# Another order of the side work in an attention unit, and the softmax shift on VectorE

## The chip, the cores and the metric

The kernel runs on one core of one Trainium2 chip. The time is the device time of one execution in microseconds; the figure that counts is the median of several runs. A core has five engines with a queue each: TensorE (PE in the profile; its weight loads are PEld), VectorE (DVE), ScalarE (ACT), GpSimd (POOL) and SyncE (SP), which here only issues DMAs. Each engine works off its own queue in order, and waits at the head of the queue until what the next instruction needs is there.

## The reference

One transformer-like block on x of 256 tokens by 2048 features, in float32:

```python
h = _rmsnorm(x, norm1_g)
proj = h @ w_in                        # q (12 heads), k and v (4 heads), u (512)
a = _rmsnorm(_window_attention(q, k, v, sink), attn_out_g)
f = _rmsnorm(_fourier_mix(u, w_fourier), fourier_out_g)
x = x + jnp.concatenate([a, f], axis=-1) @ w_out
x = x + _conv_ffn(_rmsnorm(x, norm2_g), w_up, dw_w, dw_b, w_down)
return _rmsnorm(x, normf_g)
```

Three query heads share one key head. The softmax of a head has one further logit, the head's `sink`, that takes part in the maximum and in the sum but weighs no value:

```python
scores = jnp.where(valid, q @ k.T * HEAD_DIM ** -0.5 - slope * abs(rel), NEG_INF)
m = jnp.maximum(jnp.max(scores, axis=-1, keepdims=True), sink_b)
p = jnp.exp(scores - m)
p = p / (jnp.sum(p, axis=-1, keepdims=True) + jnp.exp(sink_b - m))
out = p @ v
```

## The kernel before, in words

**Products in two parts.** Every weight block of 1 MB is loaded by SP (`load`, L161), then split (`split`, L174): ScalarE writes the high part `hi` (L181), VectorE the rest `lo` = raw - hi (L182), and TensorE multiplies the parts. Split runs two blocks ahead of TensorE; there are three raw buffers and three of each part, and the load of block i+3 is issued by SP behind the split of block i.

**Units.** One weight block is one *unit* of work. `unit(i)` (L382) writes, in this order: the small products set down in `before[i]` and the unit's 32 or 24 large matmuls on TensorE; the side work `beside[i]` on the other engines; the split of block i+2 (`step`, L362); and the side work `behind[i]`. The tables are filled by `at(...)`, and what is entered first for a unit is written first. The schedule is manual: the order in which the program is written is the order in each engine's queue. Units 0 to 3 are u, 4 to 7 v, 8 to 23 q and k (`QK_ORDER`: k0, q0, q1, q2, k1, q3, ... q11, so units 8, 12, 16 and 20 are keys), 24 to 39 the output projection. Then come the feed-forward units, which the change does not touch.

**One query head's way** (loop at L762; a head's unit is n = 0):

- n = 1, `qk_out` (L629): ScalarE copies the second half of the unit's PSUM bank (`tmp_q`, L631), VectorE adds the halves (`add_q`, L633); a key's sum is also scaled (`add_k`, L635). `qk_parts` (L638): ScalarE writes the high part of `qT` (L269) or `kT` (L643), VectorE the low part (L270, L644).
- n = 2, `scores` (L649): six matmuls `ps_s` on TensorE, ahead of the unit's own. `scores_out` (L662): VectorE adds the distances and takes each row's maximum in one instruction per half (L670); GpSimd makes the exponentials' shift in two (L674, L675). Then, in `behind`, `exps` (L678): ScalarE's two exponentials (L684) and the sink's (L688), and GpSimd's sum (L689).
- n = 3, `weigh` (L692): VectorE's reciprocal (L694) and two scalings (L697). For heads 0 to 9 also `flip_out` (L720): VectorE transposes 32 by 32 blocks (L314), and SP writes them to HBM in four DMAs.
- n = 4, `flip_in` (L726): SP reads them back, turned (`flop`). For heads 10 and 11 instead `turn` (L699) on TensorE and `turn_out` (L710).
- n = 6, `flip_parts` (L731): the probabilities `pt` in two parts, on ScalarE (L739) and VectorE (L740).
- n = 7 (heads 10 and 11: 5), `values` (L743): matmuls `ps_o`, ahead of the unit's own; `values_out` (L757): ScalarE's square (L486) and high part `cat` (L269), VectorE's low part (L270), GpSimd's running sum of squares (L490).

So the side work of one unit serves up to five heads at different stages. Since a key's unit takes the place of a query's once in four, units with i mod 4 = 2 have no scores and no `flip_parts`, and those with i mod 4 = 3 no `weigh` and no `values_out`.

Before the change the side work of a unit stands in this order: `flip_parts`, `weigh` and `flip_out`, `flip_in`, `qk_out`, `values_out`, `turn_out`, `scores_out`, `qk_parts`; then the split, then `exps`.

Of the kernel before, what the change touches and what calls it, by code (L numbers as in the profile page):

```python
# [8 lines left out]
F32 = mybir.dt.float32  # L9
F32R = mybir.dt.float32r  # L10
AF = mybir.ActivationFunctionType
ALU = mybir.AluOpType

P = 128
# [4 lines left out]
NH = 12  # L19
# [19 lines left out]
V_G2, V_GA, V_GF, V_DW, V_DB, V_SINK = 0, 16, 28, 32, 161, 204  # L39
V_N = 216  # L40


def slopes():
    def pow2(n):
        start = 2.0 ** (-8.0 / n)
        return [start ** (i + 1) for i in range(n)]

    return pow2(8) + pow2(16)[0::2][: NH - 8]
# [7 lines left out]
FLIPS = range(NH - 2)  # L56
# [48 lines left out]
def block_kernel(  # L105
# [19 lines left out]
    nc = tc.nc  # L125
    SL = slopes()
# [9 lines left out]
    def bank(pool, name):  # L136
        return pool.tile([P, 512], F32, tag=pool.name, name=name)
# [62 lines left out]
    rel = cat_pool.tile([P, 512], F32, tag="cat", name="rel")  # L200
# [16 lines left out]
    def u_part(k, o, n, m=1):  # L217

        rows = ux[k // 4][:, (k < 4) * U_HEAD :].rearrange("p (k c) -> p k c", k=4)
        return rows[:, k % 4 : k % 4 + m, o : o + n]  # L220
# [39 lines left out]
    ps = bank(dn, "ps_warm")  # L260
# [3 lines left out]
    def vcol(o, n=1):  # L264
        return vec[:, o : o + n]
# [107 lines left out]
    before, beside, behind = {}, {}, {}  # L373

    def at(when, i, f, *a):
        when.setdefault(i, []).append((f, a))
# [17 lines left out]
    for k in range(NK):  # L394
# [3 lines left out]
        n = 1 if c < 2 else 2  # L398
# [3 lines left out]
        if q % n == 0:  # L402
            w, h = u_part(k, 0, FW, n), hi[:, q : q + n, :]
# [20 lines left out]
    ph = pa.enter_context(tc.tile_pool(name="pa", bufs=1))  # L424
# [5 lines left out]
    rq_neg = ph.tile([P, 2], F32, tag="rq_neg", name="rq_neg")  # L430
    rq_pos = ph.tile([P, 2], F32, tag="rq_pos", name="rq_pos")
    rq_inv = ph.tile([P, 2], F32, tag="rq_inv", name="rq_inv")
    sink_neg = ph.tile([P, NH], F32, tag="sink_neg", name="sink_neg")

    def token_sums(c):
        for b in range(2):
# [150 lines left out]
    def distances():  # L587

        for b in range(2):
            s = slice(b * S, (b + 1) * S)  # L590
            nc.vector.tensor_scalar(rel[:, s], rel[:, s], rq_inv[:, b : b + 1], None, ALU.mult)
        nc.vector.tensor_scalar(sink_neg, vcol(V_SINK, NH), -1.0, None, ALU.mult)

    at(beside, 5, fourier_positions)
    at(before, 6, fourier_weights)
# [3 lines left out]
    at(beside, 7, fourier_rows_out)  # L599
    at(beside, 8, lambda: rows_out(v_hi, v_lo, ps_v))  # L600
    at(behind, 8, distances)

    def fourier_channels_steps():
# [22 lines left out]
    qk_sb, st = {}, {}  # L626
    sq_a = ph.tile([P, S], F32, tag="sq", name="sq_a")

    def qk_out(kind, h, ps):  # L629
        tmp = ph.tile([P, S], F32, tag="tmp", name=f"tmp_{kind}{h}", bufs=2)  # L630
        nc.scalar.activation(tmp, ps[:, S : 2 * S], AF.Copy)  # L631
        add = ph.tile([P, S], F32, tag="add", name=f"add_{kind}{h}", bufs=2)
        nc.vector.tensor_tensor(add, ps[:, 0:S], tmp, ALU.add)  # L633
        if kind == "k":
            nc.vector.tensor_tensor(add, add, r1b, ALU.mult)  # L635
        st["add", kind, h] = add
# [25 lines left out]
    def scores_out(h):  # L662

        ps = st.pop(("s", h))
        sc = ph.tile([P, 512], F32, tag="sc", name=f"sc{h}", bufs=4)
        mx = ph.tile([P, 2], F32, tag="mx", name=f"mx{h}", bufs=2)
        neg = ph.tile([P, 2], F32, tag="neg", name=f"neg{h}", bufs=2)
        for b in range(2):
            s = slice(b * S, (b + 1) * S)
            nc.vector.tensor_tensor_reduce(  # L670
                sc[:, s], ps[:, s], rel[:, s], -float(SL[h]), -3e38, ALU.add,
                ALU.max, mx[:, b : b + 1],
            )
        nc.gpsimd.tensor_tensor(neg, mx, rq_neg, ALU.mult)  # L674
        nc.gpsimd.tensor_scalar(neg, neg, sink_neg[:, h : h + 1], None, ALU.min)  # L675
        st["sc", h] = sc, neg

    def exps(h):  # L678
# [83 lines left out]
    for i in range(N_QK, N_OUT + 8):  # L762
        heads = {i - s: h for (kind, h), s in slot_of.items() if kind == "q"}
        new = [kh for kh, s in slot_of.items() if i - s == 1]
        for n, h in sorted(heads.items()):
            if n == 5 + 2 * (h in FLIPS):
                at(before, i, values, h)
        if 4 in heads and heads[4] not in FLIPS:
            at(before, i, turn, heads[4])
        if 2 in heads:  # L770
            at(before, i, scores, heads[2])
        if 6 in heads and heads[6] in FLIPS:
            at(beside, i, flip_parts, heads[6])
        if 3 in heads:
            at(beside, i, weigh, heads[3])
            if heads[3] in FLIPS:
                at(beside, i, flip_out, heads[3])
        if 4 in heads and heads[4] in FLIPS:
            at(beside, i, flip_in, heads[4])
        for kind, h in new:  # L780
            at(beside, i, lambda k=kind, h=h: qk_out(k, h, st.pop(("ps", k, h))))
        for n, h in sorted(heads.items()):
            if n == 5 + 2 * (h in FLIPS):
                at(beside, i, values_out, h)
        if 4 in heads and heads[4] not in FLIPS:
            at(beside, i, turn_out, heads[4])
        if 2 in heads:
            at(beside, i, scores_out, heads[2])
        for kind, h in new:
            at(beside, i, qk_parts, kind, h)  # L790
        if 2 in heads:
            at(behind, i, exps, heads[2])

# [85 lines left out]
    for n, (c, kq) in enumerate(OUT_ORDER):  # L879
        i = N_OUT + n  # L880
# [14 lines left out]
        if kq >= 2:  # L895
            part = "a" if kq == 2 else "f"
            ps = ps_a[c] if kq < 3 else ps_a[c, "f"]
# [315 lines left out]
    for q in range(2):  # L1213
        kind, j = items[q]
        ps = bank(mm, f"ps_{kind}{j}")
# [15 lines left out]
    for n, it in enumerate(items):  # L1231
# [8 lines left out]
        if it[0] in ("gate", "val"):  # L1240
            kind, j = it
            ps = bank(mm, f"ps_{kind}{j}")
# [4 lines left out]
        if it[0] == "product":  # L1247
            kind, g, c, p = it
# [3 lines left out]
            elif end and p in ("P2", "N4"):  # L1252
                ps = joined[c, p] = bank(mm, f"ps_{p}{g}{c}")
                by_parts(ps, parts[p], *halves.pop(it), GROUPS[g][1], True, False)
            else:
                ps = bank(mm, f"ps_{p}{g}{c}")
# [5 lines left out]
        else:  # L1262
            kind, c = it
            hi, lo = halves.pop(up_index[n])
            if c < 2:
                ps = [joined.pop((c, p)) for p in ("P2", "N4")]
            else:
                ps = [bank(mm, f"ps_l{c}{b}") for b in range(2)]
# [10 lines left out]
    i = up_index[n]  # L1279
# [158 lines left out]
```

## Time and profile before

| what | value |
|---|---|
| median of 3 runs | 941.33 us (941.06 to 941.93) |
| profiled execution | 941.03 us, its span 938.9 us |
| mean granted TensorE clock | 0.997 |
| busy share of the span: PE, DVE, ACT, POOL | 99%, 82%, 57%, 8% |
| attention's query and key units (8 to 23) | from 53.6 to 158.5 us of the span |

The span goes from the first to the last instruction of the profiled execution; the device time has about 2 us around it. The profile's views used here: the page with busy times and the chain that ended last; the waits (which engine stood still for whom); the timeline (instructions in order of time, with the idle time before them in brackets and what ended it); groups of instructions by line and shape (busy time, mean ns of one, idle time before); and windows (busy time of each engine in a stretch).

### The profile page before, as it was taken

To read this page: it belongs to the slowest core of one execution; us is meant where nothing else is said; L and a number is where in the kernel's file an instruction comes from. 1 tells how busy PE (TensorE), PEld (TensorE's weight loads), DVE (VectorE), ACT (ScalarE), POOL (GpSimd) and SP (SyncE) were. 2 spreads that over 40 slices of the span, in tenths; PEclk is the share of its full clock that TensorE was granted. 3 is DMA by queue.
4 is the path that set the end of the run, shared out by engine and by line. 5 is a ranking of instruction groups with operands and counts; after the bars stand their busy time and mean duration, and the time that the engine had idled before them with its cause. 6 is when DMAs were issued, how large, how long until landed. Compare 5 with 4: busy or idle time off the path is not lost.

```text
span 938.9 us, 12849 instructions
## 1 busy us (share of the span) xinstructions
PE 928.0 (99%) x5005; PEld 803.5 (86%) x5005; DVE 765.5 (82%) x945; ACT 539.6 (57%) x672; POOL 72.9 (8%) x104
## 2 busy tenths in 40 slices
PE   9999999999999999999999999999999999999996
PEld 7888888888888888888888888888888888888885
DVE  7657888778677777798888997878979789989986
ACT  7755666645554555566555665556655556655553
POOL 0102222300000000000000000000000000000002
PEclk9999999999999999999999999999999999999998
DMA  9965767557757668887797778777787978779652
GB/s 367 309 224 169 231 196 236 193 174 281 243 221 232 177 227 238 278 269 239 220 296 252 246 216 286 237 262 232 260 248 240 309 224 269 241 233 273 194 179 90
DMA packets 55148, 223.25 MB, mean 238 GB/s; under 512 B 21136, under 2 KB 25744, under 8 KB 31536
## 3 DMA queue, kind: packets, MB, share of 16 engines
q1 hardware_dynamic: 50544, 192.94, 56.8%
q0 software_dynamic: 4544, 29.49, 16.9%
q8 instruction: 39, 0.64, 0.3%
q14 instruction: 21, 0.17, 0.1%
HBM read 216.13 MB, written 6.29 MB: 237 GB/s over the span
## 4 chain that ended last, share of the span: by engine, by line
PE 95%; DVE 2%; ACT 1%; issue 1%; DMA 0%; POOL 0%; DVEq 0%; POOLq 0%; ACTq 0%
PE ps_val L350 25%; PE ps_gate L350 25%; PE ps_q L350 5%; PE ps_P L1148 3%; PE ps_P L1149 3%; PE ps_P L1147 3%; PE ps_N L1148 3%; PE ps_N L1149 3%; PE ps_N L1147 3%; PE ps_k L350 2%; PE ps_a L333 2%; PE ps_a L335 2%; PE ps_a L334 2%; PE ps_s L654 1%; PE ps_ff L333 1%; PE ps_ff L335 1%
## 5 line engine op out<-in xcount | busy, mean ns | idle before, releaser
L182 DVE TENSOR_TENSOR lo<-raw,hi 128x2048 fp32r<-128x2048 f32 (+1 forms) x129 | 293.5, 2275 | 53.9 <-ACT hi L181 53.6
L181 ACT ACTIVATE hi<-raw 128x2048 fp32r<-128x2048 f32 (+1 forms) x129 | 245.3, 1902 | 36.7 <-PE ps_a L334 14.6
L350 PE MATMUL ps_val<-hU,hi 128*128 128x512 f32 x688 | 236.2, 389 | 0.0
L350 PE MATMUL ps_gate<-hU,hi 128*128 128x512 f32 x688 | 236.2, 389 | 0.0
L350 PE MATMUL ps_val<-hU,lo 128*128 128x256 f32 x688 | 189.9, 276 | 0.0
L350 PE MATMUL ps_gate<-hU,lo 128*128 128x256 f32 x688 | 189.9, 276 | 0.0
L350 PEld LDWEIGHTS ps_gate<-hU,hi 128*128 128x128 f32 x688 | 129.1, 188 | 26.8
L350 PEld LDWEIGHTS ps_val<-hU,hi 128*128 128x128 f32 x688 | 129.1, 188 | 26.8
L350 PEld LDWEIGHTS ps_gate<-hU,lo 128*128 128x128 f32 x688 | 129.1, 188 | 1.3
L350 PEld LDWEIGHTS ps_val<-hU,lo 128*128 128x128 f32 x688 | 129.1, 188 | 1.3
L922 ACT ACTIVATE ft_g<-ps_gate 128x256 f32<-128x256 f32 x43 | 16.5, 384 | 123.0 <-PE ps_gate L350 123.0
L922 ACT ACTIVATE ft_v<-ps_val 128x256 f32<-128x256 f32 x43 | 16.5, 384 | 91.5 <-PE ps_val L350 91.5
L350 PE MATMUL ps_q<-hT,hi 128*128 128x512 f32 x192 | 65.1, 391 | 0.0
L1147 PE MATMUL ps_P<-hi_P,op_P 128*128 128x512 f32 x144 | 56.0, 389 | 0.0
L1148 PE MATMUL ps_P<-hi_P,op_P 128*128 128x512 f32 x144 | 56.0, 389 | 0.0
L1149 PE MATMUL ps_P<-lo_P,op_P 128*128 128x512 f32 x144 | 56.0, 389 | 0.0
L350 PE MATMUL ps_q<-hT,lo 128*128 128x256 f32 x192 | 51.2, 277 | 0.0
L1039 DVE TENSOR_TENSOR lo_N<-sumw,hi_N 128x2048 fp32r<-128x2048 f32 (+1 forms) x20 | 41.5, 2077 | 9.4 <-ACT hi_N L1038 9.2
L1147 PE MATMUL ps_N<-hi_N,op_N 128*128 128x512 f32 x108 | 42.0, 389 | 0.0
L1148 PE MATMUL ps_N<-hi_N,op_N 128*128 128x512 f32 x108 | 42.0, 389 | 0.0
L1149 PE MATMUL ps_N<-lo_N,op_N 128*128 128x512 f32 x108 | 42.0, 389 | 0.0
L350 PEld LDWEIGHTS ps_q<-hT,hi 128*128 128x128 f32 x192 | 35.2, 188 | 6.6
(389 smaller groups left out, 1598.9 us busy)
## 6 DMA issues: line engine op xcount, KB each, us to landing
raw<-in_w_up SPq DMA_DIRECT2D x86, 1024.0 KB, 5.6
raw<-in_w_in SPq DMA_DIRECT2D x20, 1024.0 KB, 5.3
raw<-in_w_out SPq DMA_DIRECT2D x16, 1024.0 KB, 4.9
sumw<-in_w_down POOLq DMA_DIRECT2D x16, 1024.0 KB, 8.7
raw<-in_w_down_late SPq DMA_DIRECT2D x4, 1024.0 KB, 7.0
raw<-in_w_down_last SPq DMA_DIRECT2D x4, 768.0 KB, 4.2
turnp<-flip SPq DMA_DIRECT2D x40, 64.0 KB, 2.9
flop<-turnp SPq DMA_DIRECT2D x10, 256.0 KB, 4.7
```

The source lines that it names most:

```text
L181: nc.scalar.activation(hi[:, 0:n], raw[:, 0:n], AF.Copy)
L182: nc.vector.tensor_tensor(lo[:, 0:n], raw[:, 0:n], f32(hi[:, 0:n]), ALU.subtract)
L333: nc.tensor.matmul(ps, ah, wh, start=first and q == q0, stop=False)
L334: nc.tensor.matmul(ps, al, wh, start=False, stop=False)
L335: nc.tensor.matmul(ps, ah, wl, start=False, stop=last and q == q0 + len(kk) - 1)
L350: nc.tensor.matmul(ps[:, x], (hi, lo)[i][:, k * P : (k + 1) * P], hk(k)[:, x], start=n == 0 and k == 0, stop=n == len(order) - 1 and k == ...
L654: nc.tensor.matmul(ps[:, b * S : (b + 1) * S], qT[:, qo + b * P : qo + (b + 1) * P], kT[:, ko : ko + S], start=n == 0, stop=n == 2,)
L922: nc.scalar.activation(tmp, ps[:, S : 2 * S], AF.Copy)
L1039: nc.vector.tensor_tensor(lo, src, f32(hi), ALU.subtract)
L1147: nc.tensor.matmul(ps, o[:, 0, p, :], hi[:, s], start=first and p == 0, stop=False)
L1148: nc.tensor.matmul(ps, o[:, 1, p, :], hi[:, s], start=False, stop=False)
L1149: nc.tensor.matmul(ps, o[:, 0, p, :], lo[:, s], start=False, stop=last and p == n - 1)
```

## The change

Three things are changed, all in the attention units.

- The order of the side work becomes: `qk_out`, `flip_parts`, `qk_parts`, `values_out`, `weigh` and `flip_out`, `flip_in` or `turn_out`, `scores_out`; then, as before, the split and `exps`.
- The running maximum of the scores begins with the sink's logit, divided by the row's query scale once at the setup (`sink_least`, two products of 12 columns in `distances`, in place of the negated sinks), and no longer with -3e38.
- The shift `neg` is then the maximum times `rq_neg`, one VectorE instruction; GpSimd's product and its minimum with the negated sink are gone.

```diff
-    sink_neg = ph.tile([P, NH], F32, tag="sink_neg", name="sink_neg")
+    sink_least = [ph.tile([P, NH], F32, tag="sink0", name="sink0"), vcol(V_N, NH)]
...
-        nc.vector.tensor_scalar(sink_neg, vcol(V_SINK, NH), -1.0, None, ALU.mult)
+        for b in range(2):
+            nc.vector.tensor_scalar(
+                sink_least[b], vcol(V_SINK, NH), rq_inv[:, b : b + 1], None, ALU.mult
+            )
...
             nc.vector.tensor_tensor_reduce(
-                sc[:, s], ps[:, s], rel[:, s], -float(SL[h]), -3e38, ALU.add,
-                ALU.max, mx[:, b : b + 1],
+                sc[:, s], ps[:, s], rel[:, s], -float(SL[h]), sink_least[b][:, h : h + 1],
+                ALU.add, ALU.max, mx[:, b : b + 1],
             )
-        nc.gpsimd.tensor_tensor(neg, mx, rq_neg, ALU.mult)
-        nc.gpsimd.tensor_scalar(neg, neg, sink_neg[:, h : h + 1], None, ALU.min)
+        nc.vector.tensor_tensor(neg, mx, rq_neg, ALU.mult)
...
+        for kind, h in new:
+            at(beside, i, lambda k=kind, h=h: qk_out(k, h, st.pop(("ps", k, h))))
         if 6 in heads and heads[6] in FLIPS:
             at(beside, i, flip_parts, heads[6])
+        for kind, h in new:
+            at(beside, i, qk_parts, kind, h)
+        for n, h in sorted(heads.items()):
+            if n == 5 + 2 * (h in FLIPS):
+                at(beside, i, values_out, h)
         if 3 in heads:
             at(beside, i, weigh, heads[3])
             if heads[3] in FLIPS:
                 at(beside, i, flip_out, heads[3])
-        if 4 in heads and heads[4] in FLIPS:
-            at(beside, i, flip_in, heads[4])
-        for kind, h in new:
-            at(beside, i, lambda k=kind, h=h: qk_out(k, h, st.pop(("ps", k, h))))
-        for n, h in sorted(heads.items()):
-            if n == 5 + 2 * (h in FLIPS):
-                at(beside, i, values_out, h)
-        if 4 in heads and heads[4] not in FLIPS:
-            at(beside, i, turn_out, heads[4])
+        if 4 in heads:
+            at(beside, i, flip_in if heads[4] in FLIPS else turn_out, heads[4])
         if 2 in heads:
             at(beside, i, scores_out, heads[2])
-        for kind, h in new:
-            at(beside, i, qk_parts, kind, h)
```

## The prediction

> **What bounds the kernel now.** I read the page first (busy times, then the chain that ended last), then the waits of TensorE, then the timeline of the attention stage engine by engine.
>
> ```profile
> span 938.9 us, 12849 instructions
> PE 928.0 (99%) x5005; PEld 803.5 (86%) x5005; DVE 765.5 (82%) x945; ACT 539.6 (57%) x672; POOL 72.9 (8%) x104
> PE 95%; DVE 2%; ACT 1%; issue 1%; DMA 0%; POOL 0%; DVEq 0%; POOLq 0%; ACTq 0%
> PE ps_s L654 <- ACT qT L269: 1.4, 2, 0.9
> ACT qT L269 <- DVE add_q L633: 27.4, 12, 3.0
> ```
>
> The reader is to see that TensorE is busy for 99% of the span and is 95% of the chain: time is saved only where TensorE itself stands still. The fourth line is the one wait for another engine that it has in the middle of the program: twice the scores (ps_s) wait for the high part of qT, 1.4 us. The fifth says why: ScalarE, which writes that part, waits in front of it for VectorE's sum add_q in each of 12 heads. A matmul that waits inside a group is merged into the group's length, so the chain in order of time has to be read too:
>
> ```profile
> 90.26 5.58 PE ps_q L350 x32
> 95.83 1.11 PE ps_s L654 x6
> 96.94 5.48 PE ps_q L350 x32
> 102.42 0.72 PE ps_o L749 x6
> 103.14 0.72 PE ps_s L654 x6
> ...
> 129.60 0.72 PE ps_o L749 x6
> ...
> 157.07 0.72 PE ps_o L749 x6
> ```
>
> The columns are start, length and what ran. Six score matmuls take 0.72 us undisturbed (103.14) and 1.11 at 95.83. In the timeline of TensorE two more groups are long, 1.19 and 1.20 us, with pure idle time in front, in brackets. These three are the scores of heads 3, 6 and 9, the first query head of each later key group, ahead of units 15, 19 and 23. VectorE's and ScalarE's rows in unit 18 then show how it comes about:
>
> ```profile
> 122.94 1.19 PE L654 MATMUL ps_s<-kT,qT 128*128 128x256 f32 x6 [0.54 <-ACT qT L269]
> 150.43 1.20 PE L654 MATMUL ps_s<-kT,qT 128*128 128x256 f32 x6 [0.85 <-ACT qT L269]
> ```
> ```profile
> 117.93 2.29 DVE L182 TENSOR_TENSOR lo<-raw,hi 128x2048 fp32r<-128x2048 f32 x1 [0.87 <-ACT hi L181]
> 120.31 0.17 DVE L694 RECIPROCAL ex<-sm 128x2 f32<-128x2 f32 x1
> 120.51 0.86 DVE L697 TENSOR_SCALAR sc<-sc,ex 128x256 f32<-128x256 f32 x2
> 121.41 0.71 DVE L314 STREAM_TRANSPOSE flip<-sc 128x512 f32<-128x512 f32 x1
> 122.05 0.39 DVE L633 TENSOR_TENSOR add_q<-ps_q,tmp_q 128x256 f32<-128x256 f32 x1
> 122.36 0.47 DVE L270 SCALAR_TENSOR_TENSOR cat<-ps_o,vec,cat 128x256 fp32r<-128x256 f32 x1
> 122.92 0.42 DVE L270 SCALAR_TENSOR_TENSOR qT<-add_q,qT 128x256 fp32r<-128x256 f32 x1
> 124.72 2.29 DVE L182 TENSOR_TENSOR lo<-raw,hi 128x2048 fp32r<-128x2048 f32 x1 [1.38 <-ACT hi L181]
> ```
> ```profile
> 119.16 0.36 ACT L631 ACTIVATE tmp_q<-ps_q 128x256 f32<-128x256 f32 x1
> 122.47 0.42 ACT L269 ACTIVATE qT<-add_q 128x256 fp32r<-128x256 f32 x1 [2.32 <-DVE add_q L633]
> ```
>
> VectorE leaves the previous unit's weight split at 120.22 (117.93 + 2.29). It then does the softmax weighting and the transpose (120.31 to 122.05) ahead of add_q, though ScalarE's copy that add_q needs has been there since 119.52. ScalarE idles 2.32 us, qT's high part starts at 122.47, the low part ends at 123.34, and TensorE, free since 122.40 (122.94 - 0.54), waits for both. Behind it, VectorE waits 1.38 us for ScalarE's `hi`, which could not start before qT.
>
> **The stall's size.** Ahead of unit 19: 0.54 + (1.19 - 0.72) = 1.01 us. Ahead of unit 23: 0.85 + (1.20 - 0.72) = 1.33. Ahead of unit 15: (1.11 - 0.72) + (5.58 - 5.48) = 0.49. Sum 2.83 us. A second way: from 102.42 to 129.60 and on to 157.07 are 27.18 and 27.47 us; four units of 5.47 with three value groups and three score groups of 0.72 need 26.2, so 1.0 and 1.3 are lost. This is all that TensorE loses in attention, 0.3% of the run.
>
> **The change part by part.**
>
> *The sum of q or k and its parts first.* Nothing is added; add_q or add_k moves ahead of weighting and transpose, and the two parts of qT or kT ahead of values_out, weighting and scores. Take unit 18 with VectorE as late as now: add_q starts at 120.22 and ends at 120.61 (0.39), the high part ends at 121.1 (0.42 and some 0.05 to hand over), the low part at 121.5. TensorE asks at 122.40, so 0.9 us are to spare. Unit 22 and unit 14 by the same steps:
>
> ```profile
> 145.41 2.29 DVE L182 TENSOR_TENSOR lo<-raw,hi 128x2048 fp32r<-128x2048 f32 x1 [0.87 <-ACT hi L181]
> 90.97 2.29 DVE L182 TENSOR_TENSOR lo<-raw,hi 128x2048 fp32r<-128x2048 f32 x1 [1.26 <-ACT hi L181]
> ```
>
> Unit 22: free at 147.70, qT whole at 149.0, asked for at 149.58 (150.43 - 0.85): 0.6 to spare. Unit 14: 93.26, 94.6, 95.83: 1.2. So all three stalls go even if nothing else gets better. **Term: -2.83 us.**
>
> What is late next? At the start of unit 19 TensorE needs scores, the values' operand and the split weights. The weights' low part for unit 19 ended at 120.22, for a start at 122.40 with a score group in front. In units 14, 18 and 22 no probabilities have to be unpacked (the head there would be a key's place), so nothing stands between. In other units the unpacking (pt) moves behind add_q, later by 0.4 us, and gates the next unit's value matmuls. In unit 19:
>
> ```profile
> 126.93 0.75 DVE L740 TENSOR_TENSOR pt<-flop,pt 128x256 fp32r<-128x256 f32 x2
> ```
>
> It ended at 127.68 and was wanted at 129.60: 1.9 to spare, 1.5 after the move.
>
> *The backlog itself.* ScalarE's `hi` now follows qT, the square and `cat`, all early, while VectorE still has weighting, transpose and scores to do. The 0.87 to 1.38 us that VectorE waits for `hi` in each unit should mostly go, so it runs less late, and the margins above grow. I take no time for this, as TensorE does not see it.
>
> *Scores' maximum last, the shift on VectorE.* Per head two GpSimd instructions go and one small VectorE product comes:
>
> ```profile
> L670 DVE CUSTOM_DVE_ANT_0 sc<-ps_s,rel 128x256 f32<-128x256 f32 x24 | 9.1, 417 | 0.0
> L674 POOL TENSOR_TENSOR neg<-mx,rq_neg 128x2 f32<-128x2 f32 x12 | 5.6, 467 | 49.0 <-DVE mx L670 49.0
> L675 POOL TENSOR_SCALAR neg<-neg,sink_neg 128x2 f32<-128x2 f32 x12 | 4.0, 332 | 1.2
> L592 DVE TENSOR_SCALAR sink_neg<-vec 128x12 f32<-128x12 f32 x1 | 0.2, 165 | 0.0
> L1183 DVE CUSTOM_DVE_ANT_0 z_P<-xs,ssq 128x256 f32<-128x256 f32 x1 | 0.5, 485 | 0.5 <-POOL ssq L1324 0.5
> 96.90:158.50 61.60, 60.20 (x374) 53.78 (x373) 50.06 (x102) 39.92 (x87) 14.37 (x26) 1.00 0.71 217
> ```
>
> The product has the shape of the reciprocal at 120.31 (two columns): 0.17 us, with the step to the next instruction 0.2. A maximum that begins with a value per row instead of a constant is not in the trace at this place; its nearest row is L1183, the same instruction begun from a column, 485 against 417 ns: 0 to 0.07 us each, two per head, and I take 0 since L1183 also reads both operands from SBUF. So VectorE gains 0.2 to 0.34 us per head, at most 12 x 0.34 = 4.1 us. The cover is in the last row (columns: span, then busy time of PE, PEld, DVE, ACT, POOL): from 96.90 to 158.50 VectorE is busy 50.06 of 61.60, so 11.5 us are free, and nine heads take 3.1 at most. **Term: 0.** If the cover were gone, the heads' 2 to 4 us would stand on the end.
>
> Behind the maximum nothing waits but ScalarE's exponentials, which come after `hi` anyway, and VectorE's split, which it reaches 0.2 us later. On GpSimd the shift needs 0.7 us and once much more:
>
> ```profile
> 170.50 2.18 POOL L674 TENSOR_TENSOR neg<-mx,rq_neg 128x2 f32<-128x2 f32 x1 [2.17 <-DVE mx L670]
> 173.10 0.60 ACT L684 ACTIVATE sc<-sc,neg,rq_pos 128x256 f32<-128x256 f32 x1 [3.61 <-POOL neg L675]
> ```
>
> There VectorE's 2.29 us split ran at the same time, and ScalarE lost 3.61 us; TensorE went on, so its removal is worth nothing by itself. The Trainium skill says why, in "SBUF — State Buffer", section "Who interferes with whom": a VectorE instruction with two SBUF inputs and a GpSimd instruction that reads SBUF exclude each other, and whichever came first holds the port to its end. This trace agrees, 2.18 us against the usual 0.31.
>
> *Weighting and transpose later in the unit.* What they feed: the transpose's four DMAs on SP, the read-back a unit later, its unpacking two units after that. SP's order within a unit stays (write, read back, then the weights' load). In unit 18 the transpose ended at 122.12; with add_q, qT (two steps) and cat in front and the same start it ends about 1.2 us later, which the smaller backlog gives back. The read-back is issued two units ahead of its use, 13.6 us by the spacing above (2 x 27.18 / 4), and lands in 4.7 (the page's DMA issues):
>
> ```profile
> flop<-turnp SPq DMA_DIRECT2D x10, 256.0 KB, 4.7
> ```
>
> For the last two heads the transposes on TensorE need the weighting: it moves behind one `cat` (0.47 us). **Term: 0.** At the setup, the negated sinks become two products of the same 12 columns, one instruction of 0.17 us more (L592) under unit 8's matmuls: 0.
>
> **Sum.** The profiled execution took 941.03 us (span 938.9 and 2.1 around it), 0.3 below the median of 941.33. 941.03 - 2.83 = 938.2; on the median, **938.5 us**. From unit 24 to the last tail TensorE shows no idle time, so what it gains here arrives at the end whole.
>
> **Rivals.**
>
> *Only part of the stalls goes.* If ScalarE, now behind the later exponentials, delivers tmp_q or qT late, one of the three stalls, or half of each, stays. For it: the margin at unit 22 is only 0.6 us if the backlog is unchanged. Against it: the backlog should shrink. Gain 0.7 to 1.9, so 939.4 to 940.6.
>
> *It does not do what it says: no gain.* If the sum is first in the program but waits at the head of VectorE's queue for ScalarE's copy, which now comes behind exponentials that wait for the new last product, the queue stands still as long as before.
>
> ```profile
> L684 ACT ACTIVATE sc<-sc,neg,rq_pos 128x256 f32<-128x256 f32 x24 | 14.0, 586 | 3.6 <-POOL neg L675 3.6
> ```
>
> Against it: the product ends before the 2.29 us split begins, and two exponentials and the copy (2 x 0.59 + 0.36 = 1.5) fit under that split. The time would be 940.8 to 941.9.
>
> *Slower: GpSimd holds VectorE up.* GpSimd's adds read SBUF, and the reordered VectorE meets them in other places:
>
> ```profile
> L490 POOL TENSOR_TENSOR sq_a<-sq_a,sq 128x256 f32<-128x256 f32 x11 | 10.2, 930 | 9.6 <-ACT sq L486 9.5
> L689 POOL TENSOR_TENSOR sm<-sm,ex 128x2 f32<-128x2 f32 x12 | 10.6, 882 | 23.9 <-ACT ex L688 23.9
> 167.32 1.30 DVE L740 TENSOR_TENSOR pt<-flop,pt 128x256 fp32r<-128x256 f32 x2
> ```
>
> The unpacking took 1.30 us beside such an add, where two of the group's 0.47 us make 0.9. VectorE has 11.5 us free in nine units, 5.1 in four, and the product takes up to 1.0 of them; with three heads per four units it becomes the bound from (5.1 - 1.0) / 3 = 1.4 us held up per head. If both GpSimd instructions of a head held it for their whole 0.93 + 0.88 = 1.81, that would be 0.4 over per head, 1.2 per group and 3.6 in three groups: 941.3 - 2.8 + 3.6 = 942.1. Against it: they overlap with such work today already, and most of 0.88 is GpSimd's own waiting. By the skill's rule named above the product, whose two inputs lie in SBUF, can be held in this way; the removal of 24 GpSimd instructions works the other way.
>
> **Chances.** Full gain (937.9 to 939.3): 0.74. Part: 0.11. No gain: 0.07. Slower: 0.08. The range takes the full case and most of the partial one: 937.9 to 940.4. About 0.2% (1.9 us) is what a measurement of this kernel can tell from no change. The full case lies beyond it, the partial and the no-gain cases within: faster 0.74, same 0.18, slower 0.08.
>
> **What would show it.** Right: six score matmuls take 0.72 us in all heads, TensorE has no wait on qT, ScalarE's 27.4 us wait on add_q falls below 10, VectorE's wait for `hi` shrinks, GpSimd has no `neg`, attention ends 2.8 us earlier and the rest keeps its length. Wrong: a new wait of TensorE on pt, lo or ps_t in units 14 to 27; L740 or L697 much longer; or a later stage that gives the time back.

## The result, and the profile after

| | median | span, median | around the span | ratio to before, 95% interval |
|---|---|---|---|---|
| before | 941.17 us of 6 runs | 938.9 (profiled run) | 2.13 | |
| changed kernel | 937.73 us of 6 runs | 935.95 | 1.80 | 0.9965 [0.9953, 0.9976] |
| changed kernel, once more | 938.28 of 5 | 936.5 | 1.78 | 0.9968 [0.9956, 0.9981] |
| before, beside that run | 941.43 of 24 | 939.3 | 2.15 | |

The change makes the kernel 0.3% faster: 3.4 us by the first medians, 3.15 by the second pair, where 2.8 was forecast. The page of the changed kernel, span, busy times and chain:

```profile
span 936.1 us, 12843 instructions
PE 926.8 (99%) x5005; PEld 802.8 (86%) x5005; DVE 767.0 (82%) x958; ACT 541.3 (58%) x672; POOL 62.2 (7%) x80
PE 98%; DVE 1%; DMA 0%; ACT 0%; issue 0%; DVEq 0%; POOLq 0%; POOL 0%; ACTq 0%
```

TensorE's share of the chain rose from 95 to 98%; VectorE's fell from 2 to 1%, those of ScalarE and "issue" from 1% to nothing. GpSimd lost 24 instructions and 10.7 us of busy time. The one wait of TensorE left (in the setup), then three waits in attention, and below them the first of these three as it was before:

```profile
PE ps_warm L262 <- POOL ones L254: 1.0, 1, 1.0
```
```profile
DVE lo L182 <- ACT hi L181: 9.1, 10, 1.6
ACT sc L686 <- DVE neg L677: 8.7, 8, 1.3
ACT qT L269 <- DVE add_q L636: 7.3, 7, 1.8
```
```profile
DVE lo L182 <- ACT hi L181: 22.5, 19, 1.6
```

The columns are the wait in all, the times it occurred and the longest. ScalarE waits 7.3 us for the sums instead of 27.4, and VectorE 9.1 us for the weights' high part instead of 22.5. ScalarE's wait for the shift, now VectorE's last small step, grew from 3.6 to 8.7 us in all; TensorE shows no wait that comes of it. The chain in order of time, the three places that were long:

```profile
53.88 5.47 PE ps_k L350 x32
...
90.51 5.58 PE ps_q L350 x32
96.09 0.72 PE ps_s L657 x6
...
122.26 0.72 PE ps_s L657 x6
...
148.42 0.72 PE ps_s L657 x6
...
154.62 0.72 PE ps_o L751 x6
```

All score groups take 0.72 us. From the first key unit to the value products ahead of unit 24, the first of the output projection, it is 154.62 - 53.88 = 100.74 us, and 157.07 - 53.62 = 103.45 before: **2.71 us less**. Unit 18 on VectorE:

```profile
114.49 2.29 DVE L182 TENSOR_TENSOR lo<-raw,hi 128x2048 fp32r<-128x2048 f32 x1
116.70 0.42 DVE L636 TENSOR_TENSOR add_q<-ps_q,tmp_q 128x256 f32<-128x256 f32 x1
117.61 0.43 DVE L270 SCALAR_TENSOR_TENSOR qT<-add_q,qT 128x256 fp32r<-128x256 f32 x1 [0.48 <-ACT qT L269]
118.24 0.48 DVE L270 SCALAR_TENSOR_TENSOR cat<-ps_o,vec,cat 128x256 fp32r<-128x256 f32 x1 [0.21 <-ACT cat L269]
```

VectorE is through with the previous split at 116.78 instead of 120.22, and qT is whole at 118.04, 4.2 us before TensorE asks (122.26). The forecast's margin with an unchanged backlog was 0.9; the other 3.3 us are the backlog that went.

### The profile page after: what moved, and what is told of

It reads as the page before. It is cut to its first block, busy times and chain, and to the rows that moved or that the text cites. A ratio compares the mean times of both kernels' runs of the same rounds, so it can differ in the third digit from the quotient of the medians.

```text
span 936.1 us, 12843 instructions
## 1 busy us (share of the span) xinstructions
PE 926.8 (99%) x5005; PEld 802.8 (86%) x5005; DVE 767.0 (82%) x958; ACT 541.3 (58%) x672; POOL 62.2 (7%) x80
## 4 chain that ended last, share of the span: by engine, by line
PE 98%; DVE 1%; DMA 0%; ACT 0%; issue 0%; DVEq 0%; POOLq 0%; POOL 0%; ACTq 0%
PE ps_val L350 25%; PE ps_gate L350 25%; PE ps_q L350 7%; PE ps_P L1149 3%; PE ps_P L1147 3%; PE ps_P L1148 3%; PE ps_N L1149 3%; PE ps_N L1147 3%; PE ps_N L1148 3%; PE ps_a L335 2%; PE ps_k L350 2%; PE ps_a L333 2%; PE ps_a L334 2%; PE ps_s L657 1%; PE ps_o L751 1%; PE ps_ff L333 1%
## 5 line engine op out<-in xcount | busy, mean ns | idle before, releaser
L181 ACT ACTIVATE hi<-raw 128x2048 fp32r<-128x2048 f32 (+1 forms) x129 | 245.5, 1903 | 36.9 <-PE ps_a L334 14.9
```

Of the source, the lines that this page charges most:

```text
L181: nc.scalar.activation(hi[:, 0:n], raw[:, 0:n], AF.Copy)
```

## The experiments

The theories: **A**, the new order frees TensorE of its wait on qT, and VectorE and ScalarE have room for the rest; the excess over 2.8 us is spread. **B**, the shift's removal from GpSimd brings part of the gain by itself. **C**, the order needs the other shift, because GpSimd's would now stand against the weight split. Every kernel was compared with runs of before on the chip that it ran on itself:

| kernel | median | span, median | around | ratio [interval] |
|---|---|---|---|---|
| e1, before again | 941.43 | 939.3 | 2.14 | 0.9999 [0.9990, 1.0008] |
| e3, order only | 943.15 | 941.35 | 1.77 | 1.0023 [1.0012, 1.0033] |
| e4, shift only | 940.86 | 939.1 | 1.76 | 0.9995 [0.9987, 1.0004] |
| e5, order, scores early, GpSimd's shift | 938.15 | 936.4 | 1.77 | 0.9962 [0.9949, 0.9976] |
| e6, changed, one product more a head | 937.99 | 936.2 | 1.79 | 0.9962 [0.9950, 0.9975] |
| e7, changed, three more | 952.91 | 951.1 | 1.80 | 1.0121 [1.0108, 1.0135] |
| e8, before, one memset more | 941.02 | 939.2 | 1.79 | 0.9996 [0.9987, 1.0005] |
| e9, sum and parts first only | 943.54 | 941.75 | 1.79 | 1.0021 [1.0011, 1.0031] |
| e10, sum first, and the shift | 937.94 | 936.15 | 1.77 | 0.9964 [0.9951, 0.9977] |

**e1 and e2: both kernels again**, unchanged.

> The kernel before, unchanged, against itself. Theory A (the change's 2.8 us come from attention, the further 0.6 us of the medians are the spread of start, tail and time around the span): its runs spread over 1 us or more, the difference from itself is within 0.5 us, and its profile has the three long score groups (1.11, 1.19, 1.20 us) again, while head, tail or the time around the span differ by some tenths from the first profile. Rival B (those 0.6 us belong to the change): its tail and its time around the span repeat to 0.1 us.

> The changed kernel once more. Theory A: ratio 0.9965 to 0.9972, 2.6 to 3.4 us faster, no wait of TensorE in attention; the stretch from the first key unit to the first output-projection unit is 2.7 us shorter than before to 0.1, the rest differs either way. Rival B: 3.3 to 3.6 us again, with tail 0.35 and time around the span 0.4 us shorter again.

Before's 11 runs spread over 1.4 us, and its score groups show 1.09, 1.20 and 1.20 us. The changed kernel's 3.15 us divide into 2.8 in the span and 0.37 around it. The figures around the span repeat to 0.06 us in both kernels, so those are not spread: on that point B's expectation held. In the tail the last wait for weights shortens in both pairs. ScalarE, the one row that shows it, first before, then the changed kernel:

```profile
912.18 1.49 ACT L1286 ACTIVATE hi<-raw 128x1536 fp32r<-128x1536 f32 x1 [2.44 <-DMA raw<-in_w_down_last]
```
```profile
909.37 1.49 ACT L1286 ACTIVATE hi<-raw 128x1536 fp32r<-128x1536 f32 x1 [2.10 <-DMA raw<-in_w_down_last]
```

This wait is 2.68 us in e1 and 2.20 in e2. In all five profiles without stalls in attention (changed kernel, e2, e5, e6, e10) it is 2.10 to 2.41 us, in all seven with stalls (before, e1, e3, e4, e7, e8, e9) 2.44 to 2.71. So some 0.3 us of the tail seem to go with the stalls and are not plain spread, as theory A had it. That is one profile for each kernel, and why the load should land sooner there stays open.

**e3: the order only.** The changed kernel with before's maximum and shift:

```diff
-                sc[:, s], ps[:, s], rel[:, s], -float(SL[h]), sink_least[b][:, h : h + 1],
-                ALU.add, ALU.max, mx[:, b : b + 1],
+                sc[:, s], ps[:, s], rel[:, s], -float(SL[h]), -3e38, ALU.add,
+                ALU.max, mx[:, b : b + 1],
             )
-        nc.vector.tensor_tensor(neg, mx, rq_neg, ALU.mult)
+        nc.gpsimd.tensor_tensor(neg, mx, rq_neg, ALU.mult)
+        nc.gpsimd.tensor_scalar(neg, neg, sink_neg[:, h : h + 1], None, ALU.min)
```

> The new order of the side work, but the maximum begins with -3e38 and the shift is GpSimd's two instructions as before. Theory A in its plain form (the order is all): the three stalls are gone, 2.7 to 2.9 us faster than before. Rival C (the two halves need each other: with the scores last the weight split follows at once, GpSimd's shift has to wait for the split's 2.3 us, ScalarE's exponentials and its next copy for the shift): the shift takes 2 us instead of 0.3 in most heads, ScalarE waits some 3 us a head for it, VectorE is 5 us or more late in units 14, 18 and 22, and the stalls stay or grow: between 1 us faster and 3 us slower than before.

It is slower than before, 1.7 us by the medians (ratio 1.0012 to 1.0033). GpSimd, VectorE and ScalarE in unit 17 of e3, three views of the timeline:

```profile
119.18 2.18 POOL L674 TENSOR_TENSOR neg<-mx,rq_neg 128x2 f32<-128x2 f32 x1 [2.22 <-DVE mx L670]
121.46 0.28 POOL L675 TENSOR_SCALAR neg<-neg,sink_neg 128x2 f32<-128x2 f32 x1
```
```profile
119.02 2.29 DVE L182 TENSOR_TENSOR lo<-raw,hi 128x2048 fp32r<-128x2048 f32 x1
123.54 0.42 DVE L633 TENSOR_TENSOR add_q<-ps_q,tmp_q 128x256 f32<-128x256 f32 x1 [2.23 <-ACT tmp_q L631]
```
```profile
121.78 0.60 ACT L684 ACTIVATE sc<-sc,neg,rq_pos 128x256 f32<-128x256 f32 x1 [3.52 <-POOL neg L675]
...
123.15 0.36 ACT L631 ACTIVATE tmp_q<-ps_q 128x256 f32<-128x256 f32 x1
```

The split starts right behind the maximum, and the first instruction of the shift takes 2.18 us, until the split's end; seven of the twelve shifts of e3 take 2.18 us. The exponentials wait for it, the next unit's copy tmp_q for the exponentials, and VectorE stands 2.23 us in front of add_q. That is a ring through three engines: from the sum of unit 16 (105.87) to that of unit 17 (114.47) to that of unit 18 (123.54) it takes 8.6 and 9.1 us where TensorE's unit takes 6.9. VectorE comes later from unit to unit in each group of four, and the stalls are back, each longer than before's:

```profile
96.91 1.20 PE L654 MATMUL ps_s<-kT,qT 128*128 128x256 f32 x6 [0.59 <-ACT qT L269]
124.47 1.20 PE L654 MATMUL ps_s<-kT,qT 128*128 128x256 f32 x6 [0.92 <-ACT qT L269]
152.63 1.22 PE L654 MATMUL ps_s<-kT,qT 128*128 128x256 f32 x6 [1.54 <-ACT qT L269]
```

C holds; A in its plain form falls. That GpSimd is held by the split itself is read from the two ending together; no run has another VectorE instruction in the split's place.

**e4: the shift only**, the other half of the diff on before's order.

> The old order, with the maximum begun with the sink's value and the shift as one VectorE product. Theory A: the three stalls stay, within 0.4 us of before, since the 0.2 to 0.34 us that VectorE gains per head fit into its wait for the weights' high part (0.87 us and more). Rival B: half a microsecond or more faster, from the tail or around the span, for 24 GpSimd instructions less.

Its three score groups take 1.08, 1.19 and 1.20 us as before, and the span is 0.2 us shorter, within the spread. The median is 0.57 us lower, but 0.39 of that lie around the span, and e8 below shows that a memset brings as much. By itself the shift's move is worth nothing, as forecast; B falls for the span.

**e5: the order without the clash.** As e3, with the scores ahead of the weighting:

```diff
+        if 2 in heads:
+            at(beside, i, scores_out, heads[2])
         if 3 in heads:
             at(beside, i, weigh, heads[3])
...
-        if 2 in heads:
-            at(beside, i, scores_out, heads[2])
```

> The new order, but the scores' maximum ahead of weighting and transpose instead of last, and the shift GpSimd's two instructions as before. Theory C (the order is right, but GpSimd's shift must not stand directly ahead of the weight split): now some 1.7 us of weighting and transpose lie between, the shift takes well under 1 us, ScalarE hardly waits for it, the three stalls are gone and attention is 2.7 us shorter than before, as in the changed kernel. Rival D (GpSimd in the chain costs by itself, or the sum first does not do it alone): at least one stall of 0.4 us or more stays.

As fast as the changed kernel with before's shift still on GpSimd. The groups of GpSimd and ScalarE in e5, then in e3:

```profile
L674 POOL TENSOR_TENSOR neg<-mx,rq_neg 128x2 f32<-128x2 f32 x12 | 2.5, 211 | 33.7 <-DVE mx L670 21.0 <-DVE ex L694 12.7
L684 ACT ACTIVATE sc<-sc,neg,rq_pos 128x256 f32<-128x256 f32 x24 | 14.2, 593 | 1.9 <-POOL neg L675 1.5
```
```profile
L674 POOL TENSOR_TENSOR neg<-mx,rq_neg 128x2 f32<-128x2 f32 x12 | 16.6, 1381 | 42.1 <-DVE mx L670 42.1
L684 ACT ACTIVATE sc<-sc,neg,rq_pos 128x256 f32<-128x256 f32 x24 | 14.2, 595 | 27.1 <-POOL neg L675 26.7
```

The same product takes 211 ns in the one place and 1381 in the other, and ScalarE waits 1.5 us instead of 26.7. It is the place ahead of the split that costs, not GpSimd. D falls.

**e6 and e7: how much VectorE can take.** The changed kernel with k = 1 or 3 products more per head, into a tile that is overwritten next:

```diff
+        for _ in range(k):
+            nc.vector.tensor_tensor(sc, rel, rel, ALU.mult)
         for b in range(2):
             s = slice(b * S, (b + 1) * S)
             nc.vector.tensor_tensor_reduce(
```

> The changed kernel with one more VectorE product of 128x512 ahead of each head's maximum, into the tile that the maximum overwrites, so the result is the same: some 0.6 us more on VectorE per head. VectorE is busy 51.9 of 59.2 us between 96.8 and 156 in the changed kernel, 7.3 free for 7 heads, 1.05 each. Theory A (VectorE is cover, not bound): as the changed kernel, within 0.3 us. Rival (VectorE is the next bound at once): 1 us or more slower than it.

> The same with three such products, some 1.8 us per head, beyond the 1.05 us that are free and beyond the 1.4 us of the prediction's slower rival. Both theories: VectorE is the bound in units 12 to 24, TensorE waits again, first for the scores of heads 3, 6 and 9; 0.8 us over for some 10 heads less what a lead of one unit swallows: 2 to 8 us slower than the changed kernel. If it is not slower by 1 us, the margin is larger than reckoned.

One product more (664 ns) costs nothing. Three cost 14.9 us against the changed kernel of the first pair, 14.6 against its repeat, more than the 2 to 8 expected. TensorE's waits in e7:

```profile
PE ps_s L657 <- ACT qT L269: 7.9, 3, 3.4
PE ps_o L753 <- DVE pt L744: 1.1, 2, 0.8
```

From the scores at 129.06 to those at 159.72, four units take 30.7 us instead of 26.2. Two things were reckoned too low. Three products take 2.1 us a head (695 ns each), not 1.8. And all of VectorE's idle time was taken as free, but with TensorE already waiting for it VectorE is still idle for 3.6 of 59.2 us (96.8 to 156), 1.2 of them waits for ScalarE. An estimate from these rows: VectorE's 22.9 us of work in four units of the changed kernel (51.9 of 59.2), 6.3 for nine products and 1.9 idle make 31.1, near the 30.7. So the next edge lies between 0.7 and 2.1 us more per head.

**e8: before with one memset more.**

```diff
     nc.vector.memset(warm, 0.0)
+    nc.vector.memset(warm, 0.0)
```

> The kernel before with one more memset of two columns at its start, nothing else. It asks what the 0.4 us around the span are, in which the kernel before (2.1 to 2.2 us) differs from the changed kernel and from both of its halves alone (1.7 to 1.8 us). If they hang on the program's making and not on what the change does, this kernel may have either figure, 1.75 would show it; if the kernel before's order and GpSimd shift together bring them, it has 2.1 to 2.2. The span stays at 939.3 to 0.6 in both.

Its span is before's, its time around the span 1.79. All nine programs that differ from before have 1.72 to 1.85 in every run, before and its copy 2.08 to 2.20. So 0.37 us of the change's gain came with each of the nine edits tried here, one of them a single memset, and have nothing to do with attention. What they are stays open.

**e9 and e10: which step of the order does it.** e9 is before with `qk_out` moved to the front and `qk_parts` behind `flip_parts`, the rest as it was; e10 is e4 with `qk_out` alone moved to the front:

```diff
+        for kind, h in new:
+            at(beside, i, lambda k=kind, h=h: qk_out(k, h, st.pop(("ps", k, h))))
         if 6 in heads and heads[6] in FLIPS:
             at(beside, i, flip_parts, heads[6])
...
-        for kind, h in new:
-            at(beside, i, lambda k=kind, h=h: qk_out(k, h, st.pop(("ps", k, h))))
```

> Of the change only this: the sum and the parts of q or k go first in the side work. The rest keeps its old order and the shift is GpSimd's as before, but with the parts gone from the end the scores' maximum is last, directly ahead of the weight split. Theory C: GpSimd's shift is held by the split (2 us instead of 0.3) as in the kernel with the order only, VectorE gets 5 us late and the stalls stay: 0 to 4 us slower than before. The prediction's step taken alone (sum and parts first remove all three stalls even with nothing else better): 2.7 us faster in the span.

> The shift on VectorE and only the sum moved to the front; the parts of q or k stay at the end of the side work as before, the other steps in the old order. Theory E (what matters is that ScalarE no longer waits for the sum, so the weights' high part is early and VectorE's backlog goes; where exactly the parts stand is of no account): the stalls are gone or under 0.2 us, attention 2.5 to 2.7 us shorter. The prediction's reckoning with the backlog unchanged: qT's low part stands behind weighting, transpose and values as now, ends near 123.3 in unit 18's terms against 122.4, and stalls of some 0.9 us stay in units 19 and 23: 0 to 1 us faster.

e9 is 2.2 us slower than before, with GpSimd's product at 1382 ns: in before the low part of q or k and VectorE's wait for `hi` lay between shift and split. e10 has the whole gain, though qT's low part stands where it stood before. VectorE in unit 18 of e10, then ScalarE's `hi` in unit 18, first before, then e10:

```profile
116.50 0.42 DVE L636 TENSOR_TENSOR add_q<-ps_q,tmp_q 128x256 f32<-128x256 f32 x1
...
118.89 0.41 DVE L270 SCALAR_TENSOR_TENSOR qT<-add_q,qT 128x256 fp32r<-128x256 f32 x1
119.22 2.28 DVE L182 TENSOR_TENSOR lo<-raw,hi 128x2048 fp32r<-128x2048 f32 x1
```
```profile
122.79 1.90 ACT L181 ACTIVATE hi<-raw 128x2048 fp32r<-128x2048 f32 x1
```
```profile
117.28 1.90 ACT L181 ACTIVATE hi<-raw 128x2048 fp32r<-128x2048 f32 x1
```

The sum starts at 116.50 (116.70 in the changed kernel); the low part is last but done at 119.30, since VectorE starts early and `hi`, 5.5 us earlier than before, no longer holds up its split here. In all of attention VectorE waits 10.8 us for `hi`, 22.5 before. Theory E holds: with the shift on VectorE, moving the one sum frees ScalarE, `hi` comes early, and VectorE's backlog goes. The parts' place is of no account in that kernel. Whether the sum alone would do it with the shift left on GpSimd was not run.

No kernel here is clearly faster than the changed one: e5, e6 and e10 lie within 0.4 us of it, and TensorE has no stall left in attention.

## Why the prediction was right or wrong, step by step

- *The bound and the stall's place*: right. TensorE's wait on qT ahead of units 15, 19 and 23 was all that attention lost, and all of it went.
- *The size, -2.83 us*: 2.71 to 2.72, the same in the changed kernel and its repeat, e5, e6 and e10 (first key unit to the value products at unit 28). The step that was off is unit 14's (5.58 - 5.48) = 0.10: that group takes 5.58 us in the changed kernel too, so it is no stall.
- *The total, 941.03 - 2.83, and with it the range's lower end, 937.9*: this is the step that put the time wrong. It changed attention alone and let all the rest stand, with "2.1 around it". Between the two profiled runs the time fell by 3.19 us, from 941.03 to 937.84: 2.71 in attention, 0.39 around the span (2.13 to 1.74) and 0.34 in the tail's last wait (2.44 to 2.10), less 0.26 by which the first key unit starts later (53.62 and 53.88). The first median, 937.73, lies 0.2 below the range. With before's 2.13 around the span, not 1.80, it would have been 938.06, inside. e8 shows that this term is not the change's doing; what it is, and why the tail's wait is shorter, stays open. The repeat's median lies 0.4 above the range's lower end, so it was partly luck on which side of it a median fell.
- *"All three stalls go even if nothing else gets better"*: the end came true, the reason given did not carry it. The step walked unit 18 with VectorE as late as now and took that lateness as given. It changes with the order: in the changed kernel VectorE is through with its split 3.4 us earlier, and with the sum and parts first and the shift left on GpSimd (e3, e9) the lateness grows by some 2 us from unit to unit where shift and split meet, and the stalls come back. No run has the new order with the lateness unchanged. The stalls go because the backlog goes.
- *"Its removal is worth nothing by itself"*: right word for word (e4), wrong as a reason to give it 0 in the sum of this change. Without it this order costs 1.7 us; with it the order gains 2.8 in the span. The two halves had to be priced together. The row that gave the price, 2.18 us at 170.50, was quoted, and the reordering makes seven of twelve shifts like that one: that step of the walk was left out. That the new time came out near the forecast all the same was luck in so far as the change held both halves.
- *The product and the maximum on VectorE*: the product takes 0.16 us, as reckoned. The maximum begun with a column takes 458 and 480 ns against 417, 0.04 and 0.06 more where 0 was taken and 0.07 bounded; e6 shows that there was room for much more.
- *Rivals.* The partial case: no stall was left. No gain, because the sum waits for ScalarE's copy, the copy for the exponentials and these for the shift: in the changed kernel that wait is 3.6 us in all (its longest 1.2) and does not reach TensorE, but with GpSimd's shift it is the ring of e3 and e9. GpSimd holding VectorE up: the unpacking and the weighting got shorter, 473 to 419 and 433 to 367 ns each. In its other direction, VectorE holding GpSimd up, the same exclusion, as far as the timing of e3 shows it, is what makes e3 and e9 slower; the forecast named it only for the kernel before.

```profile
L699 DVE TENSOR_SCALAR sc<-sc,ex 128x256 f32<-128x256 f32 x24 | 7.8, 367 | 0.4
L742 DVE TENSOR_TENSOR pt<-flop,pt 128x256 fp32r<-128x256 f32 x20 | 7.5, 419 | 0.0
L673 DVE CUSTOM_DVE_ANT_0 sc<-ps_s,rel,vec 128x256 f32<-128x256 f32 x12 | 5.8, 480 | 0.0
L673 DVE CUSTOM_DVE_ANT_0 sc<-ps_s,rel,sink 128x256 f32<-128x256 f32 x12 | 5.5, 458 | 0.0
L677 DVE TENSOR_TENSOR neg<-mx,rq_neg 128x2 f32<-128x2 f32 x12 | 1.9, 161 | 0.4
```

## What to carry to other kernels

In a queue of mixed side work, put first what another engine's in-order queue waits for: here one 0.4 us sum kept ScalarE idle, and through it VectorE, and so made both late for TensorE. When a step is moved, look at what now runs next to it: here a tiny GpSimd step directly ahead of VectorE's long split lasted as long as the split, 2.18 us against 0.2, and a ring through three engines then set the pace. Price the parts of a change together when one makes the place in which the other runs, and judge a margin of a few microseconds per unit by the backlog's growth, not by its present size.

## What the runs showed of the hardware

**TensorE's clock halved after a short stall, though not after every one.** In e3, three of eight runs have a span of 942.8 us and a mean granted clock of 0.996, the others 940.8 to 941.4 us and 0.997 to 0.998. The profiled one is of the long ones; the windows around the third stall (span, busy time of PE, PEld, DVE, ACT, POOL, then the granted clock):

```profile
150.50:153.70 3.20, 1.66 (x12) 1.25 (x11) 1.30 (x4) 2.71 (x10) 0.93 (x2) 1.00 0.96 312
153.70:157.06 3.36, 3.36 (x12) 2.78 (x11) 3.29 (x6) 2.20 (x4) 0.00 (x0) 0.50 0.27 66
157.06:160.50 3.44, 3.44 (x21) 3.04 (x20) 2.83 (x10) 2.64 (x3) 0.48 (x2) 0.99 0.88 167
```

After 1.54 us of idleness and half a microsecond's gaps within the scores, TensorE runs at half its clock for 3.4 us, which costs 1.6 us (the unit takes 7.05 us instead of 5.47): as much again as the stall. In e9's profile the same unit takes 7.04 us behind 1.70 us of idleness. Stalls of 0.9 us left the clock at 1.00 in the profiles of before and e3. But so did stalls of 1.75 and 2.66 us in e7, while its first, of 3.44 us, brought the clock to 0.50. So the length of the stall alone does not decide it. The Trainium skill, "TensorE: Matmul & The Clock Gate", section "Part 1: The HAM clock gate", says that the clock is halved after an idle window of about 3.4 us of a free-running counter and comes back after as long a busy one. The trace agrees in the half and in the 3.4 us until the clock is back. It does not agree in what sets the halving off: TensorE was busy for 1.66 of the 3.20 us ahead of it, by the first row, and 1.54 us is less than a whole idle window. Here the measurement decides; what sets it off stays open.

**A two-column GpSimd product took 0.2 or 2.2 us**, by whether VectorE's split had just begun: 211 ns on the mean in e5, 1381 in e3, where a long one ends with the split to within 0.05 us (121.36 and 121.31).
